# Early gated-MLP weights split during the input projection and kept in DRAM, and norm operations on two channel tiles at once

## The chip, the cores and the metric

The kernel runs on one core of a Trainium2 chip. The core has a tensor engine (PE), a vector engine (VectorE, DVE in the profile), a scalar engine (ScalarE, ACT), GpSimd (POOL, hardly used here) and a sync engine (SP) that issues nearly all of this kernel's DMAs. The metric is the device time of one execution in microseconds, as the median of the runs; a single profiled execution explains it.

## The reference

One encoder block on 1024 tokens with 16 meta tokens ahead, 1024 channels, all in float32. The part that matters here is the end of it:

```python
mix_out = merged @ w_out[l]
h_res = h_res + rmsnorm(mix_out, g_mix_post[l])

h2 = rmsnorm(h_res, g_ffn_pre[l])
up = centred_dwconv(h2 @ w_up[l], conv_w_ffn[l], conv_b_ffn[l])
a, v = jnp.split(up, 2, axis=-1)
ffn_out = (jax.nn.gelu(a) * v) @ w_down[l]
h_res = h_res + rmsnorm(ffn_out, g_ffn_post[l])
```

Ahead of it stand an input norm, the input projection (`w_in`, 4096 columns), a Fourier mix of one part of the columns, a short gated convolution of another, and two sigmoid gates that merge both to `merged`. `w_up` has 1024 x 5632 elements, `w_down` 2816 x 1024.

## The kernel before

Everything is transposed: channels lie on the 128 partitions, tokens along the free axis, so a "channel tile" is 128 channels by some tokens. A float32 operand is split into a high part, which ScalarE makes by a copy to the matmul format (L127), and the low rest, which VectorE subtracts (L128). A product is three matmuls, high x high, high x low and low x high (`mm3`, L159 to L163), and large products use seven block products in place of eight (class `Pair`).

The order of the work on each engine is made by a list scheduler from the dependences; `behind(...)` holds an instruction back until a named one has been placed. So the code's order is a wish, and SP's order of DMAs follows from it too. SP's queue is in order: a DMA whose buffer isn't free holds the ones behind it.

The stages that the change touches:

- **Input projection, about 140 to 297 us.** Jobs of 21 us each (gates, and the columns of the convolution) run through `run_pairs`, with `hooks[(job, step)]` called inside a job. For each of eight channel tiles kt, `transformed(kt)` loads a 256 KB block of weights (tile `wu`, L605) into one of three raw buffers of 512 KB, runs eight small matmuls on it (`wp`, L608), copies the result back into the other half of the raw buffer (L612) and stores it (`fold_d`, L613); `fold(kt)` prepares the tokens for it. The raw buffers also carry each job's weights (`C0r` and so on).
- **Merge and norms, about 400 to 577 us.** The 1040 tokens are four chunks (`CHM`: 258, 258, 258 and 256). For each chunk c, `project(c)` does the product with `w_out` (weights in rooms named `wo`), `norm_a(c)` the norm of the product and the residual sum (per channel tile: multiply by rr, L150; add xr, the input, L144; a square for the next norm, L884 on ScalarE, added up on VectorE; a store of the tile to `hres_d`, L958), and `norm_b(c)` the second norm (one scalar_tensor_tensor per channel tile, L977, in place over the stored tile) with the splits into `b11`, `b21`, `t1`, `b22`. `sums(c)` builds the operands `t2`, `t3`, `t4` of the seven-product scheme for the second half of the tokens. The tile of squares' sums goes to PE by a matmul with ones (`ms_m` for the first norm, `ms_h` for the second, L892).
- **Early products of the MLP, from about 525 us.** While the norms of later chunks run, PE takes products on what is there: two plain rows of block 0 of `w_up` (tiles `pw`, PSUM `up_z`, `up_y`) and the first products of five further blocks (tiles `ep`, PSUM `up_a`). Each needs a block of weights of 512 KB, loaded by SP (L200), split on ScalarE and VectorE. Rooms for the split parts are those of finished `wo` weights. ScalarE copies the halves out of PSUM between two products (`up_u` L290, `up_s` L1026, `up_0e` and `up_1e` L1070).
- **The up jobs from 590 us and the down projection from 970 us** come after and aren't changed.

Of the kernel before, what the change touches and what calls it, by code (L numbers as in the profile page):

```python
# [86 lines left out]
def block_kernel(ctx, tc, xT, w_u, w_in, w_fa, w_fa2, w_fb, w_fb2, w_co, w_out, w_up, w_dn,  # L87
# [17 lines left out]
    hres_d = dram.tile([P, KT, NTM], F32, name="hres_d")  # L105
    gp_d = dram.tile([P, 7, NK, HALF], F32, name="gp_d")
    early_d = dram.tile([P, len(EARLY), 2, NH], F32, name="early_d")

# [250 lines left out]
    def put(piece, kt, src, c0=0, n=NH, eng=V):  # L359
        hi, lo = piece  # L360
        split(hi[:, kt, c0 : c0 + n], lo[:, kt, c0 : c0 + n], src, eng=eng)


# [279 lines left out]
    def next_fold(kt):  # L643
# [6 lines left out]
        folded.append((xs, (hi[:, FW:w], lo[:, FW:w])))  # L650

    hooks = {(NE1 + kt, 3): lambda kt=kt: transformed(kt) for kt in range(KT)}
    for kt in range(KT):
        hooks[NE1 + kt, 5 if kt < KT - 1 else 0] = lambda kt=kt: fold(kt)
# [212 lines left out]

    def h_at(c, f):
        c0, n = CHM[c]
        return hA[f // 4][:, f % 4, c0 : c0 + n] if c < 2 else hB[:, f, c0 - 513 : c0 - 513 + n]  # L870

# [67 lines left out]
    def norm_a(c):  # L939
# [8 lines left out]
        for f in range(0, KT, 2):  # L948
            t = eo.tile([P, 2 * W], F32, tag="o", name=f"xr{c}_{f}", bufs=4)
            t = t.rearrange("p (f n) -> p f n", f=2)  # L950
            SP.dma_start(t[:, :, :v], xT[:, f : f + 2, TM + c0 : TM + c0 + v])
            xr += [t[:, i, :v] for i in range(2)]
        for f in range(KT):
            h = h_at(c, f)
            scaled = mul(h, h, rr).ins
            add(h[:, :v], h[:, :v], xr[f])
            sq.send(h)
            SP.dma_start(hres_d[:, f, c0 : c0 + v], h[:, :v])  # L958
        z[c] = sq
# [9 lines left out]
    def norm_b(c):  # L969
# [5 lines left out]
        for f in range(KT):  # L975
            h = h_at(c, f)
            V.scalar_tensor_tensor(out=h, in0=h, scalar=col("g_fpre", f), in1=rr, op0=ALU.mult, op1=ALU.mult)  # L977
            if c < 2:
                a, e = max(c0, 1), min(c0 + n, NH + 1)
                put(hx["b11" if f < 4 else "b21"], f % 4, hA[f // 4][:, f % 4, a:e], a - 1, e - a)  # L980
            elif f < 4:
                sub(A(f), h, A(f))
                put(hx["t1"], f, A(f), c0 - 513, n)
            else:
                put(hx["b22"], f - 4, B(f), c0 - 513, n)

    def second(c):
        j, n = CHM[c][0] - 513, CHM[c][1]
        return (lambda f: hA[f // 4][:, f % 4, 1 + j : 1 + j + n]), (lambda f: hB[:, f, j : j + n])

    def sums(c):
        j, n = CHM[c][0] - 513, CHM[c][1]
        A, B = second(c)
        for f in range(4):
            sub(A(f), B(f + 4), A(f))
            put(hx["t2"], f, A(f), j, n)
            sub(B(f), B(f + 4), B(f))
            sub(A(f + 4), A(f + 4), A(f))  # L1000
# [5 lines left out]
    place = {}  # L1006

    class Plain:

# [4 lines left out]
        def load(self, row, name):  # L1014
            r = room(name, F32R, f"pw{row}")
            q = [r[:, k * 512 : (k + 1) * 512] for k in range(4)]
            self.w[row] = early_pieces(f"{self.up.name}p{row}", srcs(self.up)[row], (q[:2], q[2:]))

# [119 lines left out]
    def first_blocks(*rooms_):  # L1138
        for n in rooms_:
            i = len(ep)  # L1140
            into = (None, None)
            if n is not None:
                r = room(n, F32R, f"ep{i}")
                q = [r[:, k * 512 : (k + 1) * 512] for k in range(4)]
                into = (q[:2], q[2:])
            ep.append(early_pieces(firsts[i].name, srcs(firsts[i])[0], into))

# [351 lines left out]
```

## Time and profile before

| what | value |
|---|---|
| median of 3 runs | 1219.29 us (1216.8 to 1221.27) |
| the profiled execution | 1222.5 us, span 1220.7 us |
| mean granted PE clock | 0.986 |
| busy: PE, VectorE, ScalarE | 1186.2, 1001.6, 550.6 us |
| DMA | 184.01 MB, mean 151 GB/s |
| share of the chain of waits | PE 75%, DVE 14%, DMA 7% |

A row of a view names the line, the engine, the operation and the tiles as out<-in; "x8" is a count, then come the busy time, the mean of one in ns and the idle time ahead with what ended it. In a table of windows each row is one stretch of time: its length, the busy time of PE, PEld (weight loads), DVE, ACT and POOL with their counts of instructions, the granted PE clock, the share of the DMA engines and GB/s. In the chain of waits each row has the start, the length and what it was. A timeline row has the start, the length and, in brackets, the idle time ahead and what ended it. An SP row in it is an issue, not a transfer.

### The profile page before, as it was taken

What the parts mean: (1) busy time and instruction counts of PE and PEld (TensorE: products, weight loads), DVE (VectorE), ACT (ScalarE), POOL (GpSimd) and SP (SyncE); (2) the same over time, 40 slices, a digit from 0 to 9 for tenths busy, and PEclk for the clock granted to TensorE, in tenths of its full rate; (3) what the DMA queues carried; (4) which work ended last, traced back from release to release, by engine and by line L of the source; (5) the groups of instructions that cost most, each with busy time, mean ns of one, the idle gap of its engine ahead of it and who ended that gap; (6) DMA issues with size and microseconds to landing.
All of it is one profiled execution on the core that took longest, in us unless ns stands there. A gap on an engine that the chain in (4) does not pass through costs nothing.

```text
span 1220.7 us, 22312 instructions
## 1 busy us (share of the span) xinstructions
PE 1186.2 (97%) x8822; PEld 1143.0 (94%) x8822; DVE 1001.6 (82%) x1755; ACT 550.6 (45%) x999; POOL 0.4 (0%) x6
## 2 busy tenths in 40 slices
PE   8999999999999999998999999999999999999995
PEld 7999999999999999998999999999999988888884
DVE  8999876757488866989699999989988989766678
ACT  6743333323342344656545443444344434454562
POOL 0000000000000000000000000000000000000000
PEclk9999999999999999999999999999999999999998
DMA  6336554132876757465233334323222498354433
GB/s 248 122 111 219 196 174 165 61 130 85 258 226 216 250 168 116 127 112 152 96 120 123 112 132 147 122 96 130 96 78 87 146 318 313 95 164 121 132 128 138
DMA packets 78472, 184.01 MB, mean 151 GB/s; under 512 B 7934, under 2 KB 24910, under 8 KB 78368
## 3 DMA queue, kind: packets, MB, share of 16 engines
q1 hardware_dynamic: 78224, 182.47, 47.5%
q8 instruction: 69, 1.13, 0.4%
q14 instruction: 35, 0.29, 0.1%
q10 hardware_dynamic: 144, 0.12, 0.0%
HBM read 131.30 MB, written 51.26 MB: 150 GB/s over the span
## 4 chain that ended last, share of the span: by engine, by line
PE 75%; DVE 14%; DMA 7%; issue 2%; ACT 2%; SPq 0%; DVEq 0%; ACTq 0%
PE up_d L159 3%; PE up_d L163 3%; PE up_d L161 3%; PE up_c L161 3%; PE up_c L159 3%; PE dna L159 3%; PE up_c L163 3%; PE dna L161 3%; PE dna L163 3%; PE up_a L159 3%; PE up_a L163 3%; PE up_a L161 3%; PE pq L731 2%; PE dnb L163 2%; PE dnb L161 2%; PE dnb L159 2%
## 5 line engine op out<-in xcount | busy, mean ns | idle before, releaser
L159 PE MATMUL mo<-mh,wo 128*128 128x258 f32 (+1 forms) x256 | 73.9, 289 | 0.0
L163 PE MATMUL mo<-mh,wo 128*128 128x258 f32 (+1 forms) x256 | 73.1, 285 | 0.0
L161 PE MATMUL mo<-ml,wo 128*128 128x258 f32 (+1 forms) x256 | 72.9, 285 | 0.0
L159 PEld LDWEIGHTS mo<-mh,wo 128*128 128x128 f32 x256 | 49.3, 192 | 0.2
L161 PEld LDWEIGHTS mo<-ml,wo 128*128 128x128 f32 x256 | 49.2, 192 | 0.2
L163 PEld LDWEIGHTS mo<-mh,wo 128*128 128x128 f32 x256 | 49.2, 192 | 0.0
L127 ACT CAST up_1h<-up_1t 128x512 fp32r<-128x512 f32 x11 | 6.8, 622 | 75.2 <-DVE up_1t L144 52.5
L1096 ACT ACTIVATE up_1o<-up_1x,pr 128x512 f32<-128x512 f32 x33 | 26.9, 816 | 27.9 <-DVE up_1x L144 27.5
L1100 ACT ACTIVATE up_0o<-up_0o 128x512 f32<-128x512 f32 x44 | 27.8, 631 | 24.1 <-DVE up_0o L1098 23.8
L159 PE MATMUL up_d<-b22h,up_5h 128*128 128x258 f32 (+1 forms) x168 | 34.0, 283 | 0.8 <-DVE up_1x L144 0.8
L163 PE MATMUL up_d<-b22h,up_5l 128*128 128x258 f32 (+1 forms) x168 | 34.2, 284 | 0.0
L161 PE MATMUL up_c<-t3l,up_3h 128*128 128x258 f32 (+1 forms) x168 | 34.1, 285 | 0.0
L163 PE MATMUL up_b<-t2h,up_2l 128*128 128x258 f32 (+1 forms) x168 | 34.0, 283 | 0.0
L161 PE MATMUL up_d<-b22l,up_5h 128*128 128x258 f32 (+1 forms) x168 | 33.9, 283 | 0.0
L161 PE MATMUL up_b<-t2l,up_2h 128*128 128x258 f32 (+1 forms) x168 | 33.9, 283 | 0.0
L159 PE MATMUL up_c<-t3h,up_3h 128*128 128x258 f32 (+1 forms) x168 | 33.8, 282 | 0.0
L159 PE MATMUL up_b<-t2h,up_2h 128*128 128x258 f32 (+1 forms) x168 | 33.8, 282 | 0.0
L159 PE MATMUL up_c<-t4h,up_6h 128*128 128x258 f32 (+1 forms) x168 | 33.8, 282 | 0.0
L159 PE MATMUL up_d<-t1h,up_1h 128*128 128x258 f32 (+1 forms) x168 | 33.7, 282 | 0.0
L163 PE MATMUL up_d<-t1h,up_1l 128*128 128x258 f32 (+1 forms) x168 | 33.7, 282 | 0.0
L163 PE MATMUL up_c<-t3h,up_3l 128*128 128x258 f32 (+1 forms) x168 | 33.6, 281 | 0.0
L161 PE MATMUL up_d<-t1l,up_1h 128*128 128x258 f32 (+1 forms) x168 | 33.6, 281 | 0.0
(1321 smaller groups left out, 4328.4 us busy)
## 6 DMA issues: line engine op xcount, KB each, us to landing
g<-gp_d SPq DMA_DIRECT2D x35, 512.0 KB
up_1r<-in_w_up_dram SPq DMA_DIRECT2D x22, 512.0 KB
gp_d<-up_0o SPq DMA_DIRECT2D x44, 256.0 KB
up_0r<-in_w_up_dram SPq DMA_DIRECT2D x20, 512.0 KB
s<-sig_d SPq DMA_DIRECT2D x16, 514.0 KB
sig_d<-g_s SPq DMA_DIRECT2D x30, 257.0 KB
u<-fold_d SPq DMA_DIRECT2D x8, 777.0 KB
fold_d<-fold SPq DMA_DIRECT2D x8, 521.0 KB
```

The lines of the kernel that those rows point to most:

```text
L127: a = copy(hi, src)
L159: nc.tensor.matmul(o, wh, h, start=first, stop=False, **kw)
L161: nc.tensor.matmul(o, wh, l, start=False, stop=False, **kw)
L163: newest[:] = [nc.tensor.matmul(o, wl, h, start=False, stop=last, **kw).ins]
L731: nc.tensor.matmul(o, a[:, s], b[:, ks], start=kt == n_ == ks.start == 0, stop=kt == KT - 1 and n_ == 2, skip_group_check=True,)
L1096: S.activation(t, ap[:, 1 : 1 + HALF], AF.Identity, bias=col("cb_ffn", b), scale=w(1))
L1100: S.activation(t, t, AF.Gelu_apprx_tanh)
```

## The change

Two things are changed.

First, six of the seven early weight blocks (both plain rows, and four of the five first products) are split much earlier: `ahead(i)` runs at step 1 of six jobs of the projection, loads the block (512 KB), splits it into two high and two low pieces, and stores these in a new DRAM tensor `split_d` (4 x 256 KB). In the norm stage `split_weights` then brings a block in with a single DMA of 1 MB (tile `ew`), high and low parts together, straight to its room. The seventh block is loaded and split as before.

Second, `norm_a`, the splits of `norm_b` and `sums` take two channel tiles per VectorE or ScalarE instruction (`h_two`, `put2`), with rr repeated over the two, and `norm_a` stores two tiles per DMA. The squares and the scalar_tensor_tensor of L977 remain single.

```diff
--- before.py
+++ after.py
@@ -104,6 +104,8 @@
     merged_d = dram.tile([P, KT, NT], F32, name="merged_d")
     hres_d = dram.tile([P, KT, NTM], F32, name="hres_d")
     gp_d = dram.tile([P, 7, NK, HALF], F32, name="gp_d")
+
+    split_d = dram.tile([len(EARLY) + 1, P, 4 * 512], F32, name="split_d")
     early_d = dram.tile([P, len(EARLY), 2, NH], F32, name="early_d")
 
     const = new_pool(ctx, "const")
@@ -359,6 +361,10 @@
     def put(piece, kt, src, c0=0, n=NH, eng=V):
         hi, lo = piece
         split(hi[:, kt, c0 : c0 + n], lo[:, kt, c0 : c0 + n], src, eng=eng)
+
+    def put2(piece, kt, src, c0=0, n=NH):
+        hi, lo = piece
+        split(hi[:, kt : kt + 2, c0 : c0 + n], lo[:, kt : kt + 2, c0 : c0 + n], src)
 
 
     proj_s = ExitStack()
@@ -649,7 +655,17 @@
         xs = [(hi[:, at : at + H], lo[:, at : at + H]) for at in (H, 0)]
         folded.append((xs, (hi[:, FW:w], lo[:, FW:w])))
 
+    EARLY_ROWS = [0, NF // 2, *(NF + n // 2 for n in EARLY[:-1])]
+
+    def ahead(i):
+        for n, parts in enumerate(ring.halves(f"ew{i}", w_up[EARLY_ROWS[i]])):
+            for m, t in enumerate(parts):
+                at = 512 * (2 * n + m)
+                SP.dma_start(split_d[i, :, at : at + 512], t.bitcast(F32))
+
     hooks = {(NE1 + kt, 3): lambda kt=kt: transformed(kt) for kt in range(KT)}
+    for i in range(len(EARLY_ROWS)):
+        hooks[NE1 + i, 1] = lambda i=i: ahead(i)
     for kt in range(KT):
         hooks[NE1 + kt, 5 if kt < KT - 1 else 0] = lambda kt=kt: fold(kt)
     hooks[len(jobs) - 1, 1] = lambda: next_fold(0)
@@ -866,8 +882,13 @@
         return np_.tile([P, W], F32, tag="rs", name=name, bufs=2)
 
     def h_at(c, f):
+        return h_two(c, f, 1)[:, 0]
+
+    def h_two(c, f, m=2):
         c0, n = CHM[c]
-        return hA[f // 4][:, f % 4, c0 : c0 + n] if c < 2 else hB[:, f, c0 - 513 : c0 - 513 + n]
+        if c < 2:
+            return hA[f // 4][:, f % 4 : f % 4 + m, c0 : c0 + n]
+        return hB[:, f : f + m, c0 - 513 : c0 - 513 + n]
 
     def valid(c):
         return min(CHM[c][1], NTM - CHM[c][0])
@@ -949,13 +970,14 @@
             t = eo.tile([P, 2 * W], F32, tag="o", name=f"xr{c}_{f}", bufs=4)
             t = t.rearrange("p (f n) -> p f n", f=2)
             SP.dma_start(t[:, :, :v], xT[:, f : f + 2, TM + c0 : TM + c0 + v])
-            xr += [t[:, i, :v] for i in range(2)]
-        for f in range(KT):
-            h = h_at(c, f)
-            scaled = mul(h, h, rr).ins
-            add(h[:, :v], h[:, :v], xr[f])
-            sq.send(h)
-            SP.dma_start(hres_d[:, f, c0 : c0 + v], h[:, :v])
+            xr.append(t[:, :, :v])
+        for f in range(0, KT, 2):
+            h = h_two(c, f)
+            scaled = mul(h, h, rr[:, None, :].to_broadcast([P, 2, n])).ins
+            add(h[:, :, :v], h[:, :, :v], xr[f // 2])
+            for i in range(2):
+                sq.send(h_at(c, f + i))
+            SP.dma_start(hres_d[:, f : f + 2, c0 : c0 + v], h[:, :, :v])
         z[c] = sq
         return got, scaled
 
@@ -975,27 +997,30 @@
         for f in range(KT):
             h = h_at(c, f)
             V.scalar_tensor_tensor(out=h, in0=h, scalar=col("g_fpre", f), in1=rr, op0=ALU.mult, op1=ALU.mult)
+            if f % 2 == 0:
+                continue
+            f -= 1
             if c < 2:
                 a, e = max(c0, 1), min(c0 + n, NH + 1)
-                put(hx["b11" if f < 4 else "b21"], f % 4, hA[f // 4][:, f % 4, a:e], a - 1, e - a)
+                put2(hx["b11" if f < 4 else "b21"], f % 4, hA[f // 4][:, f % 4 : f % 4 + 2, a:e], a - 1, e - a)
             elif f < 4:
-                sub(A(f), h, A(f))
-                put(hx["t1"], f, A(f), c0 - 513, n)
+                sub(A(f), h_two(c, f), A(f))
+                put2(hx["t1"], f, A(f), c0 - 513, n)
             else:
-                put(hx["b22"], f - 4, B(f), c0 - 513, n)
+                put2(hx["b22"], f - 4, B(f), c0 - 513, n)
 
     def second(c):
         j, n = CHM[c][0] - 513, CHM[c][1]
-        return (lambda f: hA[f // 4][:, f % 4, 1 + j : 1 + j + n]), (lambda f: hB[:, f, j : j + n])
+        return (lambda f: hA[f // 4][:, f % 4 : f % 4 + 2, 1 + j : 1 + j + n]), (lambda f: hB[:, f : f + 2, j : j + n])
 
 
 
     def sums(c):
         j, n = CHM[c][0] - 513, CHM[c][1]
         A, B = second(c)
-        for f in range(4):
+        for f in range(0, 4, 2):
             sub(A(f), B(f + 4), A(f))
-            put(hx["t2"], f, A(f), j, n)
+            put2(hx["t2"], f, A(f), j, n)
             sub(B(f), B(f + 4), B(f))
             sub(A(f + 4), A(f + 4), A(f))
 
@@ -1005,6 +1030,12 @@
 
     place = {}
 
+    def split_weights(i, name):
+        r = room(name, F32R, f"ew{i}")[:, : 4 * 512]
+        SP.dma_start(r.bitcast(F32), split_d[i])
+        q = [r[:, k * 512 : (k + 1) * 512] for k in range(4)]
+        return q[:2], q[2:]
+
     class Plain:
 
 
@@ -1012,9 +1043,7 @@
             self.up, self.z, self.s, self.w, self.x = up, {}, {}, {}, {}
 
         def load(self, row, name):
-            r = room(name, F32R, f"pw{row}")
-            q = [r[:, k * 512 : (k + 1) * 512] for k in range(4)]
-            self.w[row] = early_pieces(f"{self.up.name}p{row}", srcs(self.up)[row], (q[:2], q[2:]))
+            self.w[row] = split_weights(row, name)
 
         def first(self, row, part):
             if part == 0:
@@ -1138,12 +1167,10 @@
     def first_blocks(*rooms_):
         for n in rooms_:
             i = len(ep)
-            into = (None, None)
             if n is not None:
-                r = room(n, F32R, f"ep{i}")
-                q = [r[:, k * 512 : (k + 1) * 512] for k in range(4)]
-                into = (q[:2], q[2:])
-            ep.append(early_pieces(firsts[i].name, srcs(firsts[i])[0], into))
+                ep.append(split_weights(i + 1, n))
+            else:
+                ep.append(early_pieces(firsts[i].name, srcs(firsts[i])[0]))
 
     def second_half():
         hx.update(t1=act_piece(hxp, "t1", tag="t4"), t2=act_piece(hxp, "t2", tag="t2"))
```

The instructions that move stand like this. SP in the norm stage, between the loads of xr for chunk 2 and the stores of chunk 2 and 3. `hres_d<-hB` are the stores, `xr3` the input for chunk 3; `up0_0p0er` to `up1_1er` are raw weight blocks. Before:

```order
L200 DMA up0_0p0er_6361<-in_w_up_dram 128x1024
L200 DMA up0_0p1er_6397<-in_w_up_dram 128x1024
L200 DMA up0_1er_6433<-in_w_up_dram 128x1024
L200 DMA up1_1er_6507<-in_w_up_dram 128x1024
L958 DMA hres_d_61<-hB_5138 128x258 x2
L951 DMA xr3_0_6586<-in_xT_dram 128x2x255
L958 DMA hres_d_61<-hB_5138 128x258 x2
L951 DMA xr3_2_6588<-in_xT_dram 128x2x255
```

The same place now, where `ew0` to `ew3` are the blocks ready split:

```order
L1035 DMA ew0_6393<-split_d_63 128x2048
L1035 DMA ew1_6424<-split_d_63 128x2048
L980 DMA hres_d_61<-hB_5223 128x2x258 x2
L972 DMA xr3_0_6589<-in_xT_dram 128x2x255
L980 DMA hres_d_61<-hB_5223 128x2x258
L972 DMA xr3_2_6591<-in_xT_dram 128x2x255
L972 DMA xr3_4_6593<-in_xT_dram 128x2x255
L980 DMA hres_d_61<-hB_5223 128x2x258
L1035 DMA ew2_6455<-split_d_63 128x2048
L1035 DMA ew3_6524<-split_d_63 128x2048
L972 DMA xr3_6_6595<-in_xT_dram 128x2x255
L1105 DMA early_d_64<-up0_1_u_6657 128x514
```

All four weight loads stood ahead of the first store of chunk 2; now two do, and `ew2` and `ew3` stand behind its last store. The last load of xr for chunk 3 follows behind them.

SP in the second job of the projection, from the load of `wu1` on, before:

```order
L605 DMA wu1_2152<-in_w_u_dram 128x512
L391 DMA sig_d_57<-g0_2_s21_2012 128x514
L630 DMA fold_d_58<-fold5_3211 128x1042
L619 DMA fold6_3453<-in_xT_dram 128x1040
L613 DMA fold_d_58<-wu1_2152 128x512
```

And now, from the load of the block that is split ahead to the store of what wp makes:

```order
L202 DMA ew1r_2091<-in_w_up_dram 128x1024
L397 DMA sig_d_57<-g0_2_s21_2027 128x514
L636 DMA fold_d_58<-fold5_3296 128x1042
L664 DMA split_d_63<-ew1_0h_2093 128x512
L664 DMA split_d_63<-ew1_0l_2094 128x512
L664 DMA split_d_63<-ew1_1h_2097 128x512
L664 DMA split_d_63<-ew1_1l_2098 128x512
L611 DMA wu1_2181<-in_w_u_dram 128x512
L625 DMA fold6_3538<-in_xT_dram 128x1040
L619 DMA fold_d_58<-wu1_2181 128x512
```

`ew1r` stands where `wu1` stood, and `wu1` behind the four stores of its pieces. The other five jobs have the same sequence of the ew load, its four stores and the wu load.

ScalarE at the end of the norms: `t2h` and `t3h` are casts of `sums(3)`, `up_1_u` and `up_1e` copies of the early products from PSUM (the last but one), `up_0_1h` to `up_0_4h` casts for the first up job. Before:

```order
L127 CAST t3h<-hB 128x514
L127 CAST t2h<-hA_5136 128x256
L127 CAST t3h<-hB 128x514
L290 COPY up_1_u<-up_1_a 128x514
L127 CAST up_0_1h<-up_0t_7222 128x512
L127 CAST up_0_3h<-up_0r_7052 128x512
L127 CAST up_0_4h<-up_0r_7050 128x512
L127 CAST up_0_2h<-up_0t_7222 128x512
L1070 COPY up_1e<-up_1_a 128x514
```

Now:

```order
L129 CAST t3h<-hB 128x514
L129 CAST t2h<-hA_5221 128x2x256
L129 CAST t3h<-hB 128x514 x3
L129 CAST up_0_1h<-up_0t_7173 128x512
L129 CAST up_0_3h<-up_0r_7023 128x512
L129 CAST up_0_4h<-up_0r_7021 128x512
L129 CAST up_0_2h<-up_0t_7173 128x512
L292 COPY up_1_u<-up_1_a 128x514
L1099 COPY up_1e<-up_1_a 128x514
```

The copy `up_1_u` stood ahead of the four casts for the next job and now stands behind them.

## The prediction

> **What bounds the kernel now.** The page first: which engine fills the span.
>
> ```profile
> span 1220.7 us, 22312 instructions
> PE 1186.2 (97%) x8822; PEld 1143.0 (94%) x8822; DVE 1001.6 (82%) x1755; ACT 550.6 (45%) x999; POOL 0.4 (0%) x6
> ```
>
> TensorE is busy for 1186.2 of 1220.7 us. The change alters no matmul, so it can win only where PE idles or runs at a lower clock, and it can lose anywhere PE is now fed just in time. The second view is PE's waits between 470 and 620 us, the stretch that the norm and the early weights share.
>
> ```profile
> PE up_a L159 <- ACT up_u L290: 2.9, 2, 1.9
> PE ms_h L892 <- DVE sq_h L144: 2.4, 1, 2.4
> PE up_z L159 <- ACT up_s L1026: 2.2, 1, 2.2
> PE up_a L159 <- ACT up_1e L1070: 0.7, 1, 0.7
> ```
>
> Five waits, 8.2 us together; the up_a pair is 1.9 and, by subtraction, about 1.0. The third view is a table of windows of 5 us around them: after each engine's busy time stands its number of instructions, then the granted clock, the DMA share and GB/s.
>
> ```profile
> 500.00:505.00 5.00, 2.67 (x16) 2.62 (x17) 3.85 (x12) 3.92 (x13) 0.00 (x0) 0.88 0.94 215
> 505.00:510.00 5.00, 5.00 (x36) 5.00 (x36) 4.66 (x14) 3.53 (x12) 0.00 (x0) 0.78 0.55 196
> 510.00:515.00 5.00, 5.00 (x44) 4.94 (x43) 5.00 (x15) 4.76 (x14) 0.00 (x0) 1.00 0.40 155
> 545.00:550.00 5.00, 2.85 (x18) 2.64 (x17) 5.00 (x16) 3.18 (x9) 0.00 (x0) 0.82 0.39 131
> 550.00:555.00 5.00, 5.00 (x38) 5.00 (x38) 5.00 (x16) 2.97 (x8) 0.00 (x0) 0.84 0.96 147
> 555.00:560.00 5.00, 3.92 (x30) 3.35 (x28) 3.26 (x9) 2.42 (x6) 0.00 (x0) 1.00 0.91 238
> 560.00:565.00 5.00, 4.32 (x36) 4.29 (x36) 4.96 (x12) 1.86 (x4) 0.00 (x0) 1.00 0.58 171
> 575.00:580.00 5.00, 3.14 (x22) 2.94 (x22) 4.93 (x12) 4.14 (x8) 0.00 (x0) 0.89 0.15 54
> 580.00:585.00 5.00, 5.00 (x35) 5.00 (x35) 3.71 (x7) 1.38 (x4) 0.00 (x0) 0.77 0.14 53
> ```
>
> An undisturbed window holds 44 matmuls at clock 1.00 (510 to 515), 8.8 per us. The windows from 500 to 510 hold 28 and 8 too few: 36 / 8.8 = 4.1 us lost around the wait of 2.4. Of the six from 545 on, 26, 6, 14, 8, 22 and 9 are missing, 85 in all, 9.7 us. The difference to the idle times is the clock: PE looks busy from 505 to 510, at 0.78. The waits of 2.4, 2.2 and 1.9 us are followed by such a stretch; those of 1.0 and 0.7 (555 to 565) are not. So a wait of two microseconds costs nearly four.
>
> The timeline of PE places three of them, with the idle time and its releaser in brackets, and the end of the matmuls of chunk 3 that matters further below:
>
> ```profile
> 502.32 0.70 PE L892 MATMUL ms_h<-sq_h,ones 128*128 128x258 f32 x2 [2.41 <-DVE sq_h L144]
> 533.63 0.59 PE L892 MATMUL ms_m<-sq_m,ones 128*128 128x256 f32 x2
> 547.87 0.58 PE L159 MATMUL up_z<-b21h,pw 128*128 128x258 f32 x2 [2.15 <-ACT up_s L1026]
> 578.04 0.51 PE L159 MATMUL up_a<-b21h,ep 128*128 128x258 f32 x2 [1.86 <-ACT up_u L290]
> ```
>
> What ends the waits stands in the chain of waits (start, us, what), cut to the steps used below.
>
> ```profile
> 493.34 0.34 DVE rr L171
> 494.01 0.68 DVE hA L150 x2
> 499.08 0.34 DVE hA L144
> 515.00 0.60 DVE pw L128
> 518.76 0.68 DVE hB L150 x2
> 519.80 2.25 DMA hres_d<-hB
> 525.10 15.55 DMA hres_d<-hB
> 540.67 0.49 DVE hB L977
> 543.73 0.76 DVE hB L150 x2
> 551.73 7.11 DMA up_1er<-in_w_up_dram
> 560.83 4.02 DMA up_1er<-in_w_up_dram
> 576.55 0.36 ACT t2h L127
> 577.41 0.59 ACT up_u L290
> ```
>
> Wait A (502.3) ends norm_a of chunk 1: from rr on, VectorE walks 16 multiplies and adds and the squares' sums until the ms_h matmul can start. Wait B (547.9) is the up_s copy on ScalarE, queued behind squares of norm_a(3), which started only at 543.73, since norm_b(2) stood at 540.67 until a store of hB issued at 525.10 had landed, 15.55 us later. Wait C (578.0) is the up_u copy behind casts of sums(3), which VectorE feeds late. All three are VectorE's chain being late, and B is a slow transfer besides.
>
> **The change part by part.** The prices:
>
> ```profile
> L150 DVE TENSOR_TENSOR hA<-hA,rr 128x258 f32<-128x258 f32 x16 | 6.3, 424 | 0.0
> L150 DVE TENSOR_TENSOR z<-z,rr 128x512 f32<-128x512 f32 x9 | 5.8, 685 | 0.0
> L128 DVE TENSOR_TENSOR ep<-up_1er,ep 128x512 fp32r<-128x512 f32 x8 | 5.3, 686 | 1.4 <-ACT ep L127 1.4
> L127 ACT CAST ep<-up_1er 128x512 fp32r<-128x512 f32 x8 | 4.8, 620 | 2.5 <-DMA up_1er<-in_w_up_dram 2.5
> ```
>
> *Pairing.* Durations overlap in the pipeline, so the chain's step counts: two multiplies of 258 take 0.68 (494.01), 0.34 each; an instruction of 512 takes 0.60 (515.00). I take 0.60 for a pair of 516, also for the one that repeats rr, since the existing z<-z,rr of 512 costs the 685 ns that plain ones cost. A pair saves 0.08 us. There are 68 pairs: 8 in each norm_a, 4, 4, 6 and 6 in norm_b, 8 in each sums. Together 5.4 us of VectorE, of which PE sees only what lies on waits A to C.
>
> *The splits taken out.* Six blocks lose 2 subtractions each: 12 x 0.60 = 7.2 us of VectorE, and 12 casts on ScalarE. Four (pw) lie between 507 and 519, ahead of norm_a(2): 2.4 us. The eight ep fall between waits B and C.
>
> *Wait A* then shrinks by 8 x 0.08 = 0.6 us for its own multiplies and adds, and by up to 0.4 for casts queued less. So its idle falls from 2.4 to about 1.4. The half clock (4.1 - 2.4 = 1.7) may go or stay: 1.4 lies between 1.0 (none) and 1.9 (clock lost). The gain is 1.0 at least, 2.7 at most; I take 1.8. [...]
>
> *Waits B and C.* Multiplies of norm_a(2) start at 518.76 now; take away 2.4 for pw, 0.3 for pairs and 1.0 for A: about 515. Its stores were issued from 519.80 to 525.10, and now, with four DMAs for eight, from about 517 to 521. If they land like the first (2.25 us) or the 4 to 7 us of a weight load, norm_b(2) no longer stops at 540.67; with its own pairs it lets norm_a(3) start at about 536 in place of 543.73. The squares are then done some 7 us before up_s is wanted, and wait B is gone, with its half clock. The wait of 0.7 (a copy behind the casts of ep, whose raw load of 551.73 took 7.11) goes, since the pieces come ready. Wait C's casts come earlier by the 4.8 us of the eight ep subtractions and 1.1 of pairs (6 in norm_b(3), 8 in sums), but up_u now stands behind four casts of the next job too: I leave 0.7. The wait of 1.0 stays. Left are 1.0 + 0.7 + 0.4 for small gaps = 2.1 of 9.7: gain 7.6. Its ends: 9.7 if all goes, and about 1 if the transfers stay slow (below).
>
> *The splits put in.* Six times in the projection, at each job's step 1: a load of 512 KB, two casts, two subtractions, four stores of 256 KB, and only then, in the same raw buffer, the load of wu that the job's wp matmuls want.
>
> ```profile
> 167.11 0.33 SPq L605 DMA_DIRECT2D wu<-in_w_u_dram  x1
> 176.95 1.05 PE L608 MATMUL wp<-dc,wu 128*128 128x128 f32 x8
> 167.00:177.00 10.00, 10.00 (x86) 10.00 (x85) 3.03 (x7) 1.40 (x3) 0.00 (x0) 1.00 0.51 161
> ```
>
> VectorE (3.0 of 10 us busy) and ScalarE (1.4) have room for the added 1.2 and 1.1 us, so these cost nothing by themselves; DMA is busy for half. If a cover is lost it is wu's: the ew load goes out where wu's did, 167.11, and wp starts at 176.95, 9.8 us later. The ew load takes 4.0 (row 560.83), the split about 1.9 (cast 0.62, then two subtractions of 0.60 and their tail), SP's fourth store 0.3, and wu between 2.25 (129 KB stores) and 4.0 (512 KB): 8.5 to 10.2 us. PE loses 0 to 0.4 per job, 0.8 in six at about the middle (three of the six wp blocks also stand some 20 matmuls later in PE's order, 2 us more for wu); with loads of 7.11 us (551.73) 1.6 to 3.5 per job, which is a rival. SP's other issues behind the stores (fold's load, sig_d's stores) wait no longer than wu does.
>
> *Sum* against the profiled execution, which took 1222.5 us for its span of 1220.7: 0.8 - 1.8 - 7.6 = -8.6, thus 1213.9. The median of three is 1219.29, 3.2 below that execution, so 1210.7 on its scale. What this measurement can tell from no change is about 0.5%, 6.1 us.
>
> **The rivals.** *Slow transfers stay (S).* The room for ew2 (1 MB, wanted right after ms_m of chunk 3, now at 533.63, less 1.8 from A: near 532) is free only when wo4 is done, so SP issues it behind the four stores of chunk 2, where the old raw loads went ahead of the first. For it: a store took 15.55 us from 525.10 on. Against it: the first took 2.25, and nothing but those stores and xr is in flight with it. If such a stretch follows, ew2 lands at 537 to 539: PE waits 5 to 7 us and loses 1.7 of clock, and the stores hold norm_b(2) as well. Of the 9.7 us about 1 is won: 0.8 - 1.8 - 1 = -2, or 1217.3. [...] No run so far shows which it is.
>
> *The projection pays (R), slower than before.* One raw buffer carries ew and wu in turn. At crowded loads (7.11 us) each of six jobs loses about 2.7 us with its clock: 16 us against 9.4 won, 1222.5 - 9.4 + 16 = 1229, on the median's scale 1226. It decides from 9.4 / 6 = 1.6 us a job. Against it: DMA is half idle at that place.
>
> *The lead is given back (N).* From 620 to 700 VectorE is the fuller engine.
>
> ```profile
> 620.00:700.00 80.00, 80.00 (x670) 80.00 (x669) 79.23 (x128) 34.91 (x57) 0.00 (x0) 1.00 0.35 119
> ```
>
> If PE arrives earlier, VectorE must too. It has 7.2 + 5.4 us less to do before, so I expect it to; if it doesn't, waits come up there and about 1 us is left of the gain: 1218.
>
> **How the numbers follow.** My forecast gets 0.48 (1210.7), S 0.34, R 0.10, N 0.08. Forecast and S share the mechanism and differ in when the chunk 2 transfers land; what lies between is possible. Low end: A and B/C at their best (2.7, 9.7) and the projection at 0: 1219.3 - 12.4 = 1206.9, say 1207. High end: S without any gain of B/C, 1219.3 - 1.8 + 0.8 = 1218.3, plus the projection at the top of its own bounds, 6 x 0.4 = 2.4 in place of 0.8, and a microsecond for a longer ew2 wait: 1221. Faster by over 0.5% is most of the forecast (0.45) and the good part of S (0.05): 0.50. Slower by over 0.5% is R, 0.10. The rest, 0.40, is within.
>
> **What would show it.** Right: no wait of up_z on up_s near 548; clock 1.00 from 545 to 555 and from 580 to 585; norm_b(2) with no idle on hres_d; the first ew2 matmul behind ms_m of chunk 3 without a wait; wp with no wait on wu; ms_h of chunk 1 idle for 1.4. Wrong: a wait of PE on the DMA ew of several microseconds (S), waits of wp on wu of over 1.6 us, six times, 21 us apart (R), or new PE waits on VectorE past 620 (N). Pairs that cost over 0.68 would make the pairing itself worthless.

## The result and the profile after

The changed kernel takes 1236.99 us (median of 4 runs, 1234.7 to 1239.89) against 1218.05 us of the kernel before beside it: a ratio of 1.0154, 95% interval 1.0126 to 1.0181. It is slower by about 19 us; the forecast was 1210.7. The profiled execution took 1235.08 us, 12.6 us more than that of before; the rest of the 19 lies between each profiled execution and its median (4.5 us above it before, 1.9 below it now).

The page of the changed kernel, its span and engines:

```profile
span 1233.3 us, 22268 instructions
PE 1185.6 (96%) x8822; PEld 1141.5 (93%) x8822; DVE 1000.5 (81%) x1687; ACT 548.7 (44%) x979; POOL 0.4 (0%) x6
```

The work is the same within two microseconds on every engine (PE 1185.6 after 1186.2, VectorE 1000.5 after 1001.6, ScalarE 548.7 after 550.6: the pairs save instructions, the six splits have only moved). The span grew by 12.6 us and PE's busy time did not, so by this count the loss is idle time of PE; at half clock PE counts as busy (5.00 us with 25 matmuls at 0.50 from 550 to 555), as the windows below show. PE's waits, over the whole span:

```profile
PE up_a L161 <- DMA ew<-split_d: 10.8, 1, 10.8
PE wp L614 <- DMA wu<-in_w_u_dram: 6.2, 6, 1.7
PE up_a L161 <- ACT up_1e L1099: 3.1, 1, 3.1
PE ms_h L913 <- DVE sq_h L146: 2.4, 1, 2.4
```

Three waits are new: 10.8 us for the block ew2, 6.2 us in six pieces for wu, and 3.1 us for the copy up_1e. Waits B (up_z on up_s) and C (up_a on up_u) are gone, as forecast; wait A (ms_h) has kept its 2.4 us. Windows of 5 us around them:

```profile
505.00:510.00 5.00, 2.58 (x20) 2.31 (x19) 4.04 (x11) 3.67 (x11) 0.00 (x0) 1.00 1.04 184
510.00:515.00 5.00, 5.00 (x44) 5.00 (x44) 4.45 (x13) 3.76 (x12) 0.00 (x0) 1.00 0.65 134
530.00:535.00 5.00, 5.00 (x43) 4.94 (x42) 3.66 (x9) 3.50 (x11) 0.00 (x0) 1.00 1.11 101
535.00:540.00 5.00, 3.49 (x28) 3.09 (x26) 2.62 (x6) 2.24 (x5) 0.00 (x0) 1.00 1.20 99
540.00:545.00 5.00, 0.00 (x0) 0.00 (x0) 2.10 (x4) 1.15 (x2) 0.00 (x0) 0.64 1.01 174
545.00:550.00 5.00, 0.68 (x3) 0.71 (x4) 2.70 (x6) 0.60 (x1) 0.00 (x0) 0.50 0.78 293
550.00:555.00 5.00, 5.00 (x25) 5.00 (x25) 4.19 (x8) 0.18 (x2) 0.00 (x0) 0.50 0.12 42
570.00:575.00 5.00, 3.13 (x24) 2.93 (x24) 1.85 (x4) 1.47 (x3) 0.00 (x0) 1.00 0.80 317
575.00:580.00 5.00, 3.80 (x17) 3.80 (x18) 5.00 (x12) 1.11 (x2) 0.00 (x0) 0.55 0.66 203
580.00:585.00 5.00, 5.00 (x34) 5.00 (x34) 2.80 (x6) 2.68 (x5) 0.00 (x0) 0.76 0.53 218
```

By the count of 44 matmuls in a full window, those from 535 to 555 lack 16, 44, 41 and 19: 120 / 8.8 = 13.6 us for ew2, of which 10.8 is the wait and the rest half clock. From 570 to 585 lack 20, 27 and 10: 6.5 us for up_1e. Around wait A lack 24, 2.7 us in place of 4.1, since the clock stayed at 1.00 from 510 on. With 6.2 for wu that is 29.0 us where the kernel before lost 13.8, 15.2 more; smaller waits elsewhere fell (dna on up_1x from 2.7 to 1.6 us), and the spans differ by 12.6.

The chain of waits has the transfers behind two of them, and the timeline of SP the issues (an SP row is an issue):

```profile
528.85 20.33 DMA ew<-split_d
565.09 9.93 DMA up_0r<-in_w_up_dram
575.56 0.59 ACT up_1e L1099
```

```profile
524.35 0.97 SPq L980 DMA_DIRECT2D hres_d<-hB  x2
528.39 0.37 SPq L980 DMA_DIRECT2D hres_d<-hB  x1
528.85 2.44 SPq L1035 DMA_DIRECT2D ew<-split_d  x2
```

ew2 is issued right behind the last chunk 2 store and takes 20.33 us for 1 MB. In the windows from 530 to 540 the DMA engines are full (a share of 1 and more) and move about 100 GB/s: rival S, at a higher price. The wait on up_1e has a late load behind it too: ScalarE's copy stood behind casts that waited 3.44 us for up_1er, the block that is still split in place, and for up_0r.

```profile
573.77 0.62 ACT L129 CAST up_1e_0h<-up_1er 128x512 fp32r<-128x512 f32 x1 [3.44 <-DMA up_1er<-in_w_up_dram]
```

### The profile page after: what moved, and what is told of

Read it like the earlier page. It is cut to its first block, busy times and chain, and to the rows that moved or that the text cites. A ratio compares the mean times of both kernels' runs of the same rounds, so it can differ in the third digit from the quotient of the medians.

```text
span 1233.3 us, 22268 instructions
## 1 busy us (share of the span) xinstructions
PE 1185.6 (96%) x8822; PEld 1141.5 (93%) x8822; DVE 1000.5 (81%) x1687; ACT 548.7 (44%) x979; POOL 0.4 (0%) x6
## 4 chain that ended last, share of the span: by engine, by line
PE 73%; DVE 13%; DMA 9%; issue 2%; ACT 2%; SPq 1%; DVEq 0%; ACTq 0%
PE up_a L161 3%; PE up_a L165 3%; PE up_a L163 3%; PE up_d L161 3%; PE up_d L165 3%; PE up_d L163 3%; PE up_c L163 3%; PE up_c L161 3%; PE up_c L165 3%; PE dna L161 3%; PE dna L165 3%; PE dna L163 3%; PE pq L747 2%; PE dnb L163 2%; PE dnb L165 2%; PE dnb L161 2%
```

## The experiments

Eighteen kernels, each timed beside the kernel before on its own chip; the ratio to that is the number to compare, with its 95% interval.

| run | kernel | median us | ratio to before |
|---|---|---|---|
| e1 | pairs alone | 1221.43 | 1.003 (1.0013 to 1.0047) |
| e2 | early split alone | 1232.95 | 1.0112 (1.0083 to 1.0142) |
| e3 | changed, own buffers for the split | 1229.77 | 1.0088 (1.0051 to 1.0125) |
| e4 | changed, ew2's room free earlier | 1237.27 | 1.0144 (1.0108 to 1.0181) |
| e5 | changed, ew on another queue | 1235.15 | 1.0136 (1.0099 to 1.0174) |
| e6 | changed, hres_d aligned | 1220.98 | 1.0006 (0.9982 to 1.003) |
| e7 | changed, no chunk 2 stores | 1231.22 | 1.0095 (1.0062 to 1.0128) |
| e8 | before, hres_d aligned | 1210.23 | 0.9936 (0.9912 to 0.9959) |
| e9 | e6 and one cast held back | 1219.72 | 1.0014 (0.9991 to 1.0037) |
| e10 | e9 and own buffers | 1208.96 | 0.9915 (0.9885 to 0.9945) |
| e11 | e1, hres_d aligned | 1209.71 | 0.9918 (0.9889 to 0.9946) |
| e12 | before, rows 1088 apart | 1209.96 | 0.9923 (0.9894 to 0.9952) |
| e13 | e12, shifted by 4 bytes | 1209.07 | 0.9978 (0.9966 to 0.9991) |
| e14 | e10, two more casts held back | 1207.43 | 0.9959 (0.9939 to 0.9978) |
| e15 | e14, early_d aligned | 1205.89 | 0.9953 (0.9938 to 0.9968) |
| e16 | e13 again | 1210.86 | 0.9918 (0.9887 to 0.995) |
| e17 | before, hres_d with longer rows | 1210.1 | 0.9903 (0.9868 to 0.9938) |
| e18 | before, rows 1028 apart | 1209.91 | 0.9917 (0.9886 to 0.9948) |

On the chip of e13 to e15 the kernel before took 1212.52 us, on the others 1217.6 to 1220.4, so ratios of these three aren't set against the rest. It is not a chip on which everything is faster: e13 and e16 are the same kernel and took 1209.07 there and 1210.86 elsewhere. So it is the kernel before that loses less there; why is not shown, since no profile of it was taken on that chip.

**Which half loses: e1 and e2.** e1 takes the splits out of the projection, e2 the pairs:

```diff
 # e1
-    for i in range(len(EARLY_ROWS)):
-        hooks[NE1 + i, 1] = lambda i=i: ahead(i)
...
-            self.w[row] = split_weights(row, name)
+            self.w[row] = early_pieces(f"{self.up.name}p{row}", srcs(self.up)[row], (q[:2], q[2:]))
...
 # e2: the kernel before with these lines
+    for i in range(len(EARLY_ROWS)):
+        hooks[NE1 + i, 1] = lambda i=i: ahead(i)
...
+            self.w[row] = split_weights(row, name)
...
```

> The changed kernel with pairs of channel tiles, but the weight blocks loaded and split in the norm stage as before: nothing is split in the projection. Theory Q (the loss is made by the early split: wu behind ew, ew2 behind the chunk 2 stores, and the up_1e copy behind a late load): no wait of wp on wu, no wait of PE on a weight load of over 2 us, 1213 to 1219 us. Theory P (the pairs themselves cost: chains of ScalarE squares between pair operations, and stores that go out in bunches and land slowly): 1226 to 1236 us, with a PE wait of over 8 us between 530 and 560.

> The kernel before with the weight blocks split in the projection and loaded in two parts, but single channel tiles. Theory Q: six waits of wp on wu of about 1 us each, a wait on ew2 of over 8 us near 540, 1230 to 1242 us. Theory P: the waits on wu stay (6 us) but the stores go out as before, so no wait on ew2 of over 3 us and 1217 to 1226 us.

e1 came out at 1221.43, a little above theory Q's range and well below theory P's: the pairs lose nothing like 19 us, but bring nothing either. PE's waits of e1 from 470 to 640:

```profile
PE up_a L161 <- ACT up_1e L1099: 3.3, 1, 3.3
PE ms_h L911 <- DVE sq_h L146: 2.2, 1, 2.2
PE up_a L161 <- ACT up_u L292: 1.9, 2, 1.3
PE up_z L161 <- ACT up_s L1055: 1.8, 1, 1.8
```

The waits of before are all there, that on up_1e longer (3.3 us for 0.7), the others a little shorter, with 68 VectorE instructions less. e2 has most of the loss (1232.95, in theory Q's range), though both signs are smaller than expected there: four waits of wp on wu, and 6.3 us on ew2 in place of over 8.

```profile
PE up_a L160 <- DMA ew<-split_d: 6.3, 1, 6.3
PE wp L609 <- DMA wu<-in_w_u_dram: 4.3, 4, 1.8
```

So the early split makes most of the loss. In e2 SP issues ew2 ahead of the last two single stores (a wait of 6.3 for 10.8); that the bunched stores of the pairs add the rest is likely, but not shown.

**wu: e3.** The raw block of the early split gets buffers of its own:

```diff
-        for n, parts in enumerate(ring.halves(f"ew{i}", w_up[EARLY_ROWS[i]])):
+        for n in range(2):
+            t = ring.tmp(f"ew{i}t{n}")[:, :512]
+            SP.dma_start(t, w_up[EARLY_ROWS[i]][:, n * 512 : (n + 1) * 512])
+            parts = ring.piece(f"ew{i}_{n}", t)
```

> The changed kernel, but the raw block that is split ahead comes in two halves into two small buffers of another pool, so that wu no longer shares its buffer. Theory Q: the six waits of wp on wu (6.2 us together) go and nothing else changes: 1229 to 1233 us, against 1237 for the changed kernel. Rival: the projection's queue was full anyway and the waits move to the next job's weights (C0, V0): 1235 to 1239 us.

1229.77, in the range: 7.2 us less than the changed kernel. Between 130 and 320 us PE waits for wu no more; what is left there is one wait that the other kernels have too:

```profile
PE pq L750 <- DVE B_s L146: 2.0, 1, 2.0
```

**ew2: e4, e5 and e7.** Three ways to bring ew2 in time. e4 frees its room earlier, so that SP issues it ahead of the chunk 2 stores; e5 puts all six loads on GpSimd's queue; e7 leaves the chunk 2 stores out (the output's tokens of chunk 2 are then computed from a residual without the mixers' part, which one copy puts there during the projection).

```diff
 # e4
-            order = (6, 7, 0, 1, 4, 5, 2, 3)
+            order = (6, 7, 4, 5, 0, 1, 2, 3)
...
-                5: lambda: first_blocks("t3h"),
+                5: lambda: first_blocks("t3h", "t3l"),
                 6: lambda: (mean_b(2), inverse(2)),
-                7: lambda: first_blocks("t3l"),
 # e5
-        SP.dma_start(r.bitcast(F32), split_d[i])
+        nc.gpsimd.dma_start(r.bitcast(F32), split_d[i])
 # e7
+    hooks[NE1 + 6, 1] = lambda: SP.dma_start(hres_d[:, :, 513:771], xT[:, :, TM + 513 : TM + 771])
...
-            SP.dma_start(hres_d[:, f : f + 2, c0 : c0 + v], h[:, :, :v])
+            if c != 2:
+                SP.dma_start(hres_d[:, f : f + 2, c0 : c0 + v], h[:, :, :v])
```

> The changed kernel, but chunk 3 takes the wo blocks in the order 6, 7, 4, 5, 0, 1, 2, 3, so that wo4's room is free 6 us earlier and ew2 is issued ahead of the four chunk 2 stores. Theory Q by the order of the queue: ew2 lands within 6 us of its issue, the wait of 10.8 us on it falls under 2 us: 1222 to 1228 us. Rival (the transfers of this stretch are slow whatever their order): ew2 comes in time but the stores land later still, norm_b(2) waits for them and PE waits for its operands: 1231 to 1238 us.

> The changed kernel, but the six ready blocks are loaded on GpSimd's DMA queue, which has nothing else, so that ew2 stands behind no store and is issued when its room is free. Theory O (the order in one queue delays ew2): it lands within 8 us of its issue, the wait of PE on it falls from 10.8 to under 3 us: 1222 to 1229 us. Theory D (the stores of chunk 2 drain slowly and hold the DMA engines themselves, whichever queue a transfer is in): ew2 still takes over 12 us, the wait stays over 7 us: 1232 to 1240 us.

> The changed kernel without the stores of chunk 2's residual in the norm stage (what the kernel reads back there is the plain input, copied once during the projection). Theory D: without these 1.05 MB the loads of xr and ew2 behind them run at over 200 GB/s, ew2 lands within 7 us, no wait on it of over 2 us, norm_b(2) waits for no store: 1218 to 1226 us. Rival (xr's loads and the doubled weight bytes fill the engines): the wait on ew2 stays over 6 us: 1230 to 1238 us.

e4's rival was right, 1237.27. The wait on ew2 is gone, and others stand in its place (PE's waits of e4, then its windows of DMA):

```profile
PE up_a L161 <- ACT up_1e L1099: 7.9, 1, 7.9
PE up_a L161 <- ACT up_u L292: 3.8, 3, 3.1
```

```profile
530.00:535.00 5.00, 5.00 (x44) 5.00 (x44) 4.39 (x11) 3.24 (x10) 0.00 (x0) 1.00 1.14 107
535.00:540.00 5.00, 5.00 (x43) 4.94 (x42) 3.33 (x9) 2.87 (x9) 0.00 (x0) 1.00 1.18 57
540.00:545.00 5.00, 5.00 (x42) 4.95 (x42) 1.86 (x5) 1.49 (x3) 0.00 (x0) 1.00 1.22 69
```

With ew2 out of the way the stores run no faster: full engines and 57 to 107 GB/s. e5 came out at 1235.15, on theory D's side: ew2 still holds PE back until 547.0 (a wait of 6.3 us, a little under the 7 that theory D gave), and in the chain a store takes 21.95 us.

```profile
PE up_a L161 <- DMA ew<-split_d: 6.3, 1, 6.3
PE up_a L161 <- ACT up_1e L1099: 5.1, 1, 5.1
```

```profile
530.60 21.95 DMA hres_d<-hB
```

So the order in one queue alone isn't the cause. In e7 the stretch runs at 408 GB/s and PE waits for no ew:

```profile
535.00:540.00 5.00, 5.00 (x43) 4.94 (x42) 3.43 (x9) 3.27 (x11) 0.00 (x0) 1.00 1.03 408
```

But e7's time, 1231.22, lies above theory D's range: the waits on wu are still there (6.2 us), and the load up_0r behind the chunk 3 stores, which are stores to hres_d as well, took 12 us, so that up_1e waited 6.9 us (the chain's row and PE's wait):

```profile
557.99 12.11 DMA up_0r<-in_w_up_dram
```

```profile
PE up_a L161 <- ACT up_1e L1101: 6.9, 1, 6.9
```

I had left both out of that expectation. What e4, e5 and e7 share is that the loss in the norm stage follows the stores of hres_d.

**Why the stores are slow: e6 and e8.** hres_d had rows of 1026 tokens (that many, not 1040, are in the four chunks), 4104 bytes, the four chunks one behind the other; here each chunk's row gets 1536 bytes of its own.

```diff
-    hres_d = dram.tile([P, KT, NTM], F32, name="hres_d")
+    hres_d = dram.tile([P, KT, 4, 384], F32, name="hres_d")
...
-            SP.dma_start(hres_d[:, f : f + 2, c0 : c0 + v], h[:, :, :v])
+            lo, hi = ((2, 258), (0, 256), (1, 258), (0, 255))[c]
+            SP.dma_start(hres_d[:, f : f + 2, c, : hi - lo], h[:, :, lo:hi])
...
```

> The changed kernel, but hres_d keeps each chunk's row of a channel tile in a place of its own of 1536 bytes, so that every stored row (1020 to 1028 bytes) starts at a multiple of 512 bytes, where the rows were 4104 bytes long and chunks began at any multiple of 4; the residual is read back in two DMAs for one. Theory D with the rows' places as its cause: the chunk 2 stores land within 8 us of their issue in place of 10 to 19, ew2's wait falls under 3 us: 1221 to 1229 us. Rival (the place of a row doesn't matter, the count of about 1 KB pieces does): no change, 1234 to 1240 us.

> The kernel before with only the aligned places in hres_d. If theory D holds with the rows' places as its cause, the slow stretch from 526 to 541 goes here too: norm_b(2) no longer waits 3 us for a store, the wait of up_z on up_s and part of those behind it go: 1210 to 1215 us. If the places don't matter: 1216 to 1220 us.

Both in the range: 16 us off the changed kernel (1220.98), 8.2 us off the kernel before (1210.23). The stretch of chunk 2's stores in the kernel before (first two rows) and in e6 (last two), and PE's waits of e8 from 470 to 640:

```profile
525.00:530.00 5.00, 5.00 (x43) 4.94 (x42) 4.90 (x13) 4.58 (x14) 0.00 (x0) 1.00 1.18 124
530.00:535.00 5.00, 5.00 (x42) 4.95 (x41) 5.00 (x15) 2.25 (x6) 0.00 (x0) 1.00 1.22 112
525.00:530.00 5.00, 5.00 (x45) 5.00 (x44) 3.17 (x8) 3.51 (x10) 0.00 (x0) 1.00 1.04 355
530.00:535.00 5.00, 5.00 (x42) 4.94 (x42) 2.77 (x7) 1.87 (x5) 0.00 (x0) 1.00 0.89 361
```

```profile
PE up_a L159 <- ACT up_u L290: 1.6, 1, 1.6
PE up_a L159 <- ACT up_1e L1071: 0.7, 1, 0.7
```

e6 moves 355 and 361 GB/s where the changed kernel moved 134 and 101, and in e8 the waits A, B and C of the kernel before are gone without a single VectorE instruction less (1755 in both); an up_u wait of 1.6 us near 550 and that on up_1e are left. What the prediction had read as VectorE's chain was this tensor's stores. For wait A the link is a load behind the stores of chunk 0: ScalarE waited for mr, and the casts b11h that VectorE needs stood behind it. The kernel before, then e8:

```profile
486.56 0.71 ACT L127 CAST mh<-mr 128x256 fp32r<-128x256 f32 x2 [6.46 <-DMA mr<-merged_d]
481.84 0.71 ACT L127 CAST mh<-mr 128x256 fp32r<-128x256 f32 x2 [1.33 <-DMA mr<-merged_d]
```

The stores are not the whole loss, though. e6 and e8 ran on one chip, and with fast stores in both the changed kernel is still 10.8 us slower (1220.98 against 1210.23). About 8 of the 19 us are thus owed to the slow stores, and the rest to wu and the copy up_1e, which e10 below mends.

**What about the rows: e12, e13, e16, e17, e18.** In e6 and e8 several things changed at once: where a row starts, whether chunks follow on one another (and share a few tokens, which two chunks both stored before), and the length of the rows with the distance of the partitions (32832 bytes before, 49152 then).

```diff
 # e12: e8 with 272 in place of 384;  e13, e16: e12 with every row 1 element later
+            SP.dma_start(hres_d[:, f, c, 1 : 1 + hi - lo], h[:, lo:hi])
 # e17: the kernel before with
+    hres_d = dram.tile([P, KT, 1088], F32, name="hres_d")[:, :, :NTM]
 # e18: e8 with 257 in place of 384
```

> As e8, the kernel before with places of their own for the stored rows, but 1088 bytes apart, so that each starts at a multiple of 64 bytes and not of 512. If a start at a multiple of 64 bytes is what matters: 1208 to 1212 us, as e8. If it takes 512: chunk 2's stores land 10 us or more after their issue, 1215 to 1219 us.

> As e12, the kernel before with the stored rows 1088 bytes apart, but each row starts 4 bytes later, at no multiple of 64. If the start of a row is what makes the stores slow: chunk 2's stores land 10 us or more after their issue, 1215 to 1220 us. If it was the old layout (rows that follow on one another, so that chunks share a line): 1208 to 1212 us, as e12.

> e13 once more beside the two that follow, since the kernel before ran at 1212.5 us on the chip of e13 and at 1218 on the others. If the place of a row's start within 64 bytes matters: 0.997 or more of the kernel before, chunk 2's stores landing 8 us or more after their issue. If it doesn't: 0.992 to 0.995, landing within 5 us.

> The kernel before with nothing changed but the length of hres_d's rows, 4352 bytes in place of 4104, so that the partitions lie 34816 bytes apart and not 32832 (32768 + 64); chunks follow on one another and start at any multiple of 4, as before. If the distance of the partitions (so near a power of two) makes the stores slow: 0.992 to 0.995 of the kernel before, chunk 2's stores within 5 us. If it is the shared or split lines: 0.998 to 1.002.

> As e8, but the places are 1028 bytes long, so that the partitions lie 32896 bytes apart (32768 + 128). If the distance of the partitions matters: slow as the kernel before, 0.998 to 1.002. If a place of its own for each chunk matters: 0.992 to 0.995.

e12 held; e13's ratio told little, on a chip where the kernel before takes 1212.52, though PE's waits in the stage, 1.8 us on up_u and 0.7 on up_1e, were close to e12's 1.6 and 0.7; e16, on one where it takes 1220.36, gives 0.9918: a start at multiples of 64 bytes is not needed. e17 is one number in one line, and gives 0.9903. So the length of hres_d's rows, 4104 bytes with partitions 32832 apart, makes the stores slow; chunks that follow on one another don't. My further guess, that any distance near 32768 does it, fell with e18: 32896 is fast. Which property of 32832 (or of 4104) it is stays open: in the fast kernels the rows are multiples of 16 bytes and the partitions' distances multiples of 128, in the slow one neither, and a longer hres_d may also move the tensors behind it in DRAM; no run separates these. The row length alone was tried on the kernel before, not on the changed one. The windows of e17, whose same stretch is over by 530:

```profile
520.00:525.00 5.00, 5.00 (x44) 5.00 (x43) 5.00 (x15) 3.90 (x10) 0.00 (x0) 1.00 0.87 225
525.00:530.00 5.00, 5.00 (x43) 4.94 (x42) 4.90 (x13) 4.55 (x14) 0.00 (x0) 1.00 0.51 155
```

**What is left of the change: e9, e10, e11, e14, e15.** Casts that stand ahead of the copy up_1e are held back, and the own buffers added:

```diff
 # e9: e6 with
     with behind(*done):
         first_blocks(None)
...
-    with behind(*done):
+    with behind(firsts[3].kept):
         rest = ring.pair(ups[ORDER[0]].name, *srcs(ups[ORDER[0]]), ALL)
 # e10: e9 and e3's buffers;  e11: e1 with e6's hres_d;  e14: e10 with
-    with behind(*done):
+    with behind(firsts[3].kept):
         first_blocks(None)
 # e15: e14 with
+    early_d = dram.tile([P, len(EARLY), 2, 528], F32, name="early_d")[:, :, :, :NH]
```

> The changed kernel with the aligned places of hres_d, and the first cast for the next up job held back until the copy up_u of the third first product is placed, so that the copy up_1e of the second no longer stands behind a cast whose raw load comes late. Theory: the wait of up_a on up_1e (2.9 us) and the half clock behind it (4.4 us with the wait) go: 1215 to 1218 us, against 1221 with aligned places alone. Rival: the cast was no more than a sign of the late queue and another copy waits in its place: 1219 to 1222 us.

> As e9, and the block that is split ahead comes into small buffers of its own, as in e3. Theory: the waits of wp on wu (5 to 6 us) go as well, all three costs of the early split are gone: 1208 to 1212 us. Rival: with the norm stage in order the projection's lead is lost elsewhere: 1214 to 1218 us.

> Pairs alone (as e1) with the aligned places. If VectorE's chains set the norm stage, as the prediction had it, the 68 pairs bring 2 to 5 us over the kernel before with aligned places: 1205 to 1208 us. If they don't set it once the stores land in time: 1209 to 1213 us, the same as e8.

> As e10, and the two casts of the seventh block held back as well, so that the copy up_1e stands behind no cast that waits for a load. If these casts were what remained of that wait (2.3 us in e9, 1.1 in e10): it goes, 1206 to 1209 us. If not: 1208 to 1211 us.

> As e14, with early_d's rows of 2056 bytes at multiples of 64 bytes too (2112 apart). If rows that start elsewhere slow every store of this stage: the early_d stores that land in 4 us or more now land in about 2, 1 to 2 us less than e14. If only the bursts of hres_d mattered: the same as e14.

e9 missed its range and fell in its rival's (1219.72): the copy still stood behind the casts of the seventh block, whose raw load is late too (ScalarE's timeline of e9):

```profile
557.34 0.62 ACT L129 CAST up_1e_0h<-up_1er 128x512 fp32r<-128x512 f32 x1 [3.44 <-DMA up_1er<-in_w_up_dram]
558.38 0.58 ACT L1100 COPY up_1e<-up_a 128x514 f32<-128x514 f32 x1
```

e14 holds those back as well, and PE's waits in the stage come down to 0.9 us:

```profile
PE up_a L161 <- ACT up_1e L1103: 0.7, 1, 0.7
PE up_a L161 <- ACT up_u L292: 0.2, 1, 0.2
```

Its time, 1207.43, lies in the range, but on another chip than e10's 1208.96 and 1.5 us from it, so a gain in time isn't shown. e15's is 1205.89, but its interval overlaps e14's: whether early_d's rows matter isn't shown. e10 (0.9915, 10.8 us below e9 on one chip) came out as expected and e11 (0.9918) as the second of its two cases: with the stores fast, the changed kernel mended, pairs alone, and the kernel before with one padded tensor (0.9903 to 0.9936) can't be told apart. So even the mended change is worth nothing measurable beside the padding. e10, e11, e8, e12 and e16 to e18 all beat both kernels, by about 1% or less where the kernel before is concerned; the smallest edit among them is e17.

## Why the prediction was wrong

- **Read rightly.** PE's waits set the time, the change alters no matmul, and both B and C went. Rival S named the place (ew2 behind the chunk 2 stores), and wu behind ew was named too.
- **The step that failed first** is, on waits B and C, "If they land like the first (2.25 us) or the 4 to 7 us of a weight load, norm_b(2) no longer stops at 540.67". The row of 15.55 us stood beside that of 2.25, and I took the better for the forecast. The stores landed no sooner (the last was issued at 528.39, and norm_b(2) went on at 547.26, 18.9 us later), so norm_b(2) stopped twice (VectorE's timeline after):

```profile
541.27 0.49 DVE L999 SCALAR_TENSOR_TENSOR hB<-hB,pr,rrb 128x258 f32<-128x258 f32 x1 [3.02 <-DMA hres_d<-hB]
547.26 0.49 DVE L999 SCALAR_TENSOR_TENSOR hB<-hB,pr,rrb 128x258 f32<-128x258 f32 x1 [3.90 <-DMA hres_d<-hB]
```

  The term of -7.6 became +10 or so: 13.6 and 6.5 us lost where the kernel before lost 9.7.
- **Rival S was priced too low.** "PE waits 5 to 7 us and loses 1.7 of clock": it waited 10.8 and lost 2.8. Its arithmetic had ew2 issued near 521 and landing at 537 to 539; it was issued at 528.85, since wu had cost 6 us by then and wait A none less, and PE moved on by only those 6 us while the transfer took 20.33. Its reason, ew2's place behind the stores in one queue, wasn't the whole cause either: issued ahead (e4) ew2 came in time, but copies that came late cost PE 11.7 us in its place; on a queue of its own (e5) ew2 still cost 6.3; and with other rows (e6) PE waits for no ew2 in the same order. So the order alone doesn't set the price here.
- **wu: the right place, the sum too short.** I had 8.5 to 10.2 us for ew load, split and wu load, and 0 to 0.4 us lost a job. SP and PE after:

```profile
167.47 0.33 SPq L202 DMA_DIRECT2D ew1r<-in_w_up_dram  x1
174.66 0.40 SPq L611 DMA_DIRECT2D wu<-in_w_u_dram  x1
178.59 1.13 PE L614 MATMUL wp<-dc,wu 128*128 128x128 f32 x8 [1.32 <-DMA wu<-in_w_u_dram]
```

  From ew's issue to wu's 7.2 us, for which I had 6.2, and 3.9 more to wp, the top of my 2.25 to 4.0: 11.1, so 1.3 us lost here and 6.2 in six jobs for 0.8 (e3 confirms it with 7.2). That is above even the upper end of 10.2: by the chain of waits ew's load took 4.38 us for 4.0, and its split and stores took the rest. Taking the middle of the sum made it worse, since a loss that starts at zero only counts the late side.
- **Wait A: -1.8 forecast, -1.4 measured, for another reason.** Its idle time stayed 2.4; only the clock behind it stayed up. e8 shows what sets it: with fast stores, and mr's load no longer late behind them, it is gone without any pairing.
- **up_1e wasn't forecast.** I had followed up_u behind the casts of the next job, not its neighbour, the second copy up_1e, behind the casts that wait for the late loads of up_1er and up_0r: 6.5 us.
- **The pairs** were priced at 5.4 us of VectorE, of which PE would see a part. It saw none (e1: 1.003; e11 as e8). What set the waits was the stores, not VectorE's own work.

## What to carry to other kernels

When a short transfer takes 2 us in one row and 15 us in another (2.25 and 15.55 here), look for the reason before counting on either: here it was the row length of a DRAM tensor, and padding it (0.9903) was worth as much by itself as with any move of work around it. An engine that waits at the end of a chain isn't its cause: VectorE's lateness came from stores that an in-place operation had to wait for (3.02 and 3.90 us in the changed kernel). A load that is put in front of another in a shared buffer adds its whole length to the other's (4.38 us of the 7.2 from ew's issue to wu's), so sum the upper bounds against the deadline, leave room beyond them (here the sum came out 0.9 us above them), and follow every instruction behind one that waits, not only the one that waits now.

## What the runs showed of the hardware

With stores in pieces of about 1 KB (1032 bytes a row of 258 tokens; all packets from 518 to 540 in the kernel before, 2379, carry 2.65 MB) to a tensor with rows of 4104 bytes (partitions 32832 apart), the windows between 525 and 545 with a DMA share of 1.06 to 1.32 moved 57 to 134 GB/s in all (the kernel before, the changed one, e4 and e5); with rows of 4352 bytes (e17) the same stretch reached 225 GB/s at a share of 0.87 and was over by 530. Partitions 32896 bytes apart (e18, 0.9917) and 34816 (e17, 0.9903) were fast where 32832 was slow. A PE wait of 2.4 us cost half clock in the kernel before (0.88 and 0.78 from 500 to 510) and none in the changed one (505 to 515 at 1.00): the length of a wait alone doesn't decide it. Where half clock came in these two kernels, it came in like portions: with the lower clock at 0.50, as from 545 to 555 in the changed kernel, the windows' clocks add up to 3.4 us of it at each of the three waits of the kernel before ((0.12 + 0.22) x 5 / 0.5 at wait A), and to 6.9 us at up_1e and 13.6 at ew2 in the changed one, two and four times as much. What sets these portions was not shown.
